# Block 2: where the second half of the output weights is kept and when it and the merged rows are split

## The chip, the core and the metric

The kernel runs on one core of a Trainium2 chip. The engines are TensorE (PE, matmuls, with its weight loads PEld), VectorE (DVE), ScalarE (ACT), GpSimd (POOL) and SyncE (SP, which here issues nearly all DMAs). Each takes its own instructions in order; they meet through semaphores. The metric is the device time of one execution in microseconds. The kernel before takes 2372.64 us, the median of 3 runs (2372.11 to 2374.22).

## The reference, cut to what matters

Two blocks work on 1024 rows of 1024 numbers. The first is a two-layer hybrid of gating and sparse attention; the diff doesn't touch it. The second block normalises its input, projects it, runs a windowed attention and a short gated convolution beside each other, merges them with two gates, projects the sum, adds the input, and sends the result through a mixture of 32 experts. The part that matters is the merge and the output projection:

```python
merged = (jax.nn.sigmoid(g_attn) * (attn @ w_attn_proj[l])
          + jax.nn.sigmoid(g_conv) * (conv @ w_conv_proj[l]))
x = x + merged @ w_out[l]
h2 = rmsnorm(x, norm2_g[l])
x = x + hierarchical_moe(h2, ...)
```

All is float32, and the routing of the experts needs products that are nearly exact.

## The kernel before

Every product is made of three matmuls (`mm3`, lines 99 to 102): each operand is split into a high part, rounded to the matmul's format, and a low part, the rest. `split` (lines 104 to 111) makes the high part on ACT (line 108) or POOL (line 106) and the low part by a subtraction on DVE or POOL (line 111).

The merge (lines 1376 to 1390) runs two branches, first the convolution (`br` 0), then the attention (`br` 1), each over four column groups `dc` of 256. For each group `gate` makes the gate's projection with eight weight tiles k, and ACT turns it into tanh in `sg` (line 1363); then `dense_T(4, ...)` makes the branch's own projection. `ev_p` takes it off PSUM: for branch 0 into the sums M; for branch 1 DVE multiplies into `sg` (line 1388) and POOL adds `sg` to M (line 1389). M lies in the buffer X, one k (128 of the 1024 merged columns) after the other, transposed, so that k is the inner dimension of the output projection: column group `dc` gives k = 2 dc and 2 dc + 1.

Three kinds of place in SBUF matter. `big2` holds two places of tag "s32": first the transposed input's high and low parts, which the gates read until the last gate is through; then `mT`, the split sums of row tiles 0 to 3 and 4 to 7. `gp` has a place of tag "c32" with the split branch input `sT`, which the last projection reads, and after it `w2b`, the second half (k 4 to 7) of the split output weights. `f16` holds the first half, `w2a`, two k per branch.

`load_w2` loads the output weights in parts of one k and 512 columns (256 KB) into two buffers `w2raw`, and splits each: ACT the high, POOL the low part. The first half runs as background work: a generator in the list `bgs`, of which `bg` takes a step whenever its budget is positive; `dense_T` calls `bg` while it emits matmuls, `flush` takes all that is left. The second half is written after the merge (`run(load_w2(4, ...))`), followed by the splits of all eight row tiles, high parts on ACT for even and on POOL for odd tiles.

After that comes the output projection (lines 1550 to 1582). For row tile t it loads the input rows `xt` into a place of X where k 6 or 7 of M lay (line 1552), makes two halves of 24 matmuls each in PSUM banks "half" of which there are three, adds them on DVE (line 1560), starts loads of expert weights into freed places, stores rows, transposes the sum (line 1573) and runs the router. Then the experts follow, with their weights streamed by SP, at most three loads on the way (`AHEAD`).

What sets the order on each engine is not the program's text alone: the building library simulates the program and gives each engine a list, by priority and by its own estimate of when operands are ready. Background steps are emitted at a raised priority (`HI`). So a change in the text can move instructions on every engine behind the place of the change.

Of the kernel before, what the change touches and what calls it, by code (L numbers as in the profile page):

```python
# [11 lines left out]
FR = mybir.dt.float32r  # L12
# [7 lines left out]
OP = mybir.AluOpType  # L20
# [4 lines left out]
S = 1024  # L25
D = 1024
NT = 8
# [13 lines left out]
def tile_hybrid(ctx, tc, I, out):  # L41
    nc = tc.nc
    V, A, G, T = nc.vector, nc.scalar, nc.gpsimd, nc.tensor
# [60 lines left out]
    def split(hi, lo, src, which="pool", sub=None):  # L104
        if which == "pool":
            G.tensor_scalar(hi, src, 1.0, 0.0, op0=OP.mult, op1=OP.add)
        elif which == "act":
            A.activation(hi, src, AF.Copy)  # L108
        else:
            V.tensor_copy(hi, src)  # L110
        return (sub or V).tensor_tensor(lo, src, hi.bitcast(FT), op=OP.subtract)  # L111
# [51 lines left out]
    bgs, streams = [], []  # L163
# [15 lines left out]
    def step(q):  # L179
        try:  # L180
            with tc.high_priority(offset=HI[0]):
                ns = next(q[0])
        except StopIteration:
            q.pop(0)
            return 0.0
        ns, cost = ns if isinstance(ns, tuple) else (ns, 0.0)
        if cost and streams:
            charge(cost)
        return ns
# [32 lines left out]
    def flush(q):  # L222
        while q:
            step(q)
        due[0] = 0.0
# [18 lines left out]
    def dense_T(KT, rhs, evac, bgt=1300.0):  # L244
        ps = [bank([128, 1024], "big") for _ in range(2)]
        for k0 in range(0, KT, 2):
            hi, lo = wnext()
            for f in range(2):
                for kk in range(2):
                    k = k0 + kk  # L250
                    for h in range(2):
                        c = slice(h * 512, (h + 1) * 512)
                        mm3(ps[f][:, c], hi[:, kk, f * 128:(f + 1) * 128], lo[:, kk, f * 128:(f + 1) * 128],
                            rhs(k, 0)[:, c], rhs(k, 1)[:, c], start=(k == 0), stop=(k == KT - 1))
                if k0 + 2 == KT:
                    for h in range(2):
                        evac(f, h, ps[f][:, h * 512:(h + 1) * 512])
                bg(bgt, 12 * 512 / 2.4)
# [222 lines left out]
    def run(g):  # L481
        for _ in g:
            pass
# [638 lines left out]
    big2 = ctx.enter_context(tc.tile_pool(name="big2", bufs=2))  # L1122
# [221 lines left out]
    M = X.rearrange("p t a c -> p (t a c)").rearrange("p (k s) -> p k s", s=S)  # L1344
# [3 lines left out]
    def load_w2(k0, dst):  # L1348
        for kk in range(dst.shape[2]):
            for h in range(2):  # L1350
                raw = gp.tile([128, 512], FT, name="w2raw", bufs=2)
                nc.sync.dma_start(raw, wo2[(k0 + kk) * 128:(k0 + kk + 1) * 128, h * 512:(h + 1) * 512])
                hs = slice(h * 512, (h + 1) * 512)
                split(dst[:, 0, kk, hs], dst[:, 1, kk, hs], raw, "act", G)
                yield 2000.0
        for kk in range(dst.shape[2]):
            w2.append((dst, kk))

    def gate():
        sg = sgpool.tile([128, 2, S], FT, name="sg", tag="sg")  # L1360

        def ev_g(f, h, ps):
            A.activation(sg[:, f, h * 512:(h + 1) * 512], ps, AF.Tanh, scale=0.5)
        dense_T(8, rhs, ev_g)
        return sg

    flush(bgs)
    bank_plan(2, 0, 2, 2)
    sg = gate()
    a2.close()  # L1370
    g2 = ExitStack()
    gp = g2.enter_context(tc.tile_pool(name="gp", bufs=1))
    for br, src in enumerate((convf, attnf)):
        sT = gp.tile([128, 2, 4, S], FR, name="c32")
        for k in range(4):
            split(sT[:, 0, k, :], sT[:, 1, k, :], src[:, k, :], "act")
        bgs.append(load_w2(2 * br, f16.tile([128, 2, 2, S], FR, name="w2a", tag="f16")))
        for dc in range(4):
            if br or dc:
                sg = gate()  # L1380

            def ev_p(f, h, ps):
                hs = slice(h * 512, (h + 1) * 512)
                m = M[:, 2 * dc + f, hs]
                if br == 0:
                    V.scalar_tensor_tensor(m, sg[:, f, hs], 1.0, ps, op0=OP.add, op1=OP.mult)
                else:
                    V.scalar_tensor_tensor(sg[:, f, hs], sg[:, f, hs], 1.0, ps, op0=OP.add, op1=OP.mult)
                    G.tensor_tensor(m, m, sg[:, f, hs], op=OP.add)
            dense_T(4, lambda k, a: sT[:, a, k, :], ev_p)  # L1390
    flush(bgs)
    op = g2.enter_context(tc.tile_pool(name="op", bufs=1))
    run(load_w2(4, gp.tile([128, 2, 4, S], FR, name="w2b", tag="c32", bufs=1)))
    mT = [big2.tile([128, 4, 2, 8, 128], FR, name="s32") for _ in range(2)]
    for t in range(NT):
        m = mT[t // 4][:, t % 4]
        split(m[:, 0], m[:, 1], M[:, :, t * 128:(t + 1) * 128], "pool" if t % 2 else "act")


    h2d = dram.tile([S, D], FT, name="h2d")  # L1400
# [146 lines left out]
    raw0, s32 = [], []  # L1547
    PRE = (0, 1, 1, 1, 1, 1, 1, 1)

    for t in range(NT):  # L1550
        xt = Xf[:, 6 + t % 2]
        nc.sync.dma_start(xt, x2[t * 128:(t + 1) * 128, :])
        for h in range(2):
            hs = slice(h * 512, (h + 1) * 512)
# [159 lines left out]
    with tc.issue_after(late[4].ins):  # L1714
        V.tensor_tensor(ovx[:, 0:NLIM, :], bc(cnt[:, None, :], [128, NLIM, NE]), bc(lim[:, :, None], [128, NLIM, NE]),
                        op=OP.is_gt)
# [53 lines left out]
def build(nc, tc_cls, shapes):  # L1770
    I = {n: nc.dram_tensor(f"in_{n}_dram", a.shape, mybir.dt.from_np(a.dtype), kind="ExternalInput").ap()
         for n, a in shapes.items()}
    out = nc.dram_tensor("out_0_dram", (S, D), FT, kind="ExternalOutput").ap()
    with tc_cls(nc, schedule_with_timeline_sim=True) as tc:
        tile_hybrid(tc, I, out)
# [13 lines left out]
```

## Time and profile before

| what | value |
|---|---|
| median of 3 runs | 2372.64 us (2372.11 to 2374.22) |
| the profiled execution | 2371.94 us |
| its span, first to last instruction | 2369.8 us |
| PE busy | 2140.5 us (90%) |
| DVE busy | 1521.2 us (64%) |
| ACT, POOL busy | 1082.8 us, 1082.0 us (46% each) |
| mean granted TensorE clock | 0.961 |

The shares are means over very different stages: the first block takes most of the span, the merge lies from about 1590 to 1855 us, the output projection until 1983, the experts until the end. Times in the rows are counted from the start of the span. A line number is that of the kernel, and for a helper such as `split` it is the helper's line, so the tile names tell the place: s is any "s32" place, c a "c32" place, whi and wlo a weight tile's high and low part, big and half PSUM banks. What stands in square brackets behind a row is the engine's idle time before it and what ended it.

### The profile page before, as it was taken

Reading aid. Unit: us, or ns where it says so; the run is one execution under the profiler, and the core shown is the slowest. Engines: PE = TensorE matmul, PEld = TensorE weight load, DVE = VectorE, ACT = ScalarE, POOL = GpSimd, SP = SyncE. Lnnn points to the kernel's source line nnn. Section 1 sums busy time; section 2 is a strip of 40 time slices with the busy share of each in tenths; the row PEclk is TensorE's granted clock in tenths of the full one; section 3 lists DMA queues with packets and bytes.
Section 4 is the critical chain, followed back from the end, with each engine's and each line's share of the span. In section 5 each row is a group of like instructions: output and inputs, shape, how many; then the busy total and the mean of one; then the engine's idle time right before and its main releaser. Section 6 shows DMA issues by size and latency. Waiting matters only on the chain. (4 is left out here: it accounts for less than half of the span.)

```text
span 2369.8 us, 35974 instructions
## 1 busy us (share of the span) xinstructions
PE 2140.5 (90%) x13235; PEld 1883.9 (79%) x13235; DVE 1521.2 (64%) x3191; ACT 1082.8 (46%) x1943; POOL 1082.0 (46%) x1018
## 2 busy tenths in 40 slices
PE   5998998798989979997998999999999797999896
PEld 4898897587879979876887888888888586888785
DVE  9768887677753769685776348861010345888784
ACT  4333443554642443436554335652121222778774
POOL 4664575556736553845554345532244412222221
PEclk9999998899999989998999999999999998999998
DMA  7522112312114111223111111122121256999994
GB/s 239 188 79 86 53 32 81 106 59 68 41 47 138 45 36 49 66 67 108 68 45 41 44 41 34 30 52 67 49 67 45 98 209 200 311 325 326 317 329 116
DMA packets 146392, 260.88 MB, mean 110 GB/s; under 512 B 24681, under 2 KB 101889, under 8 KB 133905
## 3 DMA queue, kind: packets, MB, share of 16 engines
q1 hardware_dynamic: 139024, 241.59, 31.1%
q0 software_dynamic: 7168, 16.79, 3.2%
q8 instruction: 105, 1.72, 0.3%
q14 instruction: 95, 0.77, 0.1%
HBM read 228.83 MB, written 37.90 MB: 113 GB/s over the span
## 5 line engine op out<-in xcount | busy, mean ns | idle before, releaser
L111 POOL TENSOR_TENSOR wlo<-wraw,whi 128x512 fp32r<-128x512 f32 (+1 forms) x188 | 249.8, 1329 | 484.9 <-ACT whi L108 459.2
L101 PE MATMUL big<-wlo,s 128*128 128x256 f32 (+1 forms) x1536 | 440.4, 288 | 16.0 <-POOL wlo L111 16.0
L100 PE MATMUL big<-whi,s 128*128 128x256 f32 (+1 forms) x1536 | 437.8, 289 | 13.6 <-ACT s L506 8.4
L102 PE MATMUL big<-whi,s 128*128 128x256 f32 (+1 forms) x1536 | 439.6, 288 | 0.0
L101 PEld LDWEIGHTS big<-wlo,s 128*128 128x128 f32 x1536 | 301.2, 196 | 22.8 <-POOL wlo L111 19.6
L100 PEld LDWEIGHTS big<-whi,s 128*128 128x128 f32 x1536 | 298.6, 196 | 21.9 <-ACT s L506 11.0
L102 PEld LDWEIGHTS big<-whi,s 128*128 128x128 f32 x1536 | 300.6, 196 | 3.1 <-issue 0.9
L108 ACT ACTIVATE whi<-wraw 128x512 fp32r<-128x512 f32 (+1 forms) x188 | 117.7, 627 | 385.2 <-PE big L102 127.2
L111 DVE TENSOR_TENSOR ew<-s,ew 128x1024 fp32r<-128x1024 f32 x138 | 162.8, 1220 | 39.0 <-ACT ew L108 37.9
L636 DVE SCALAR_TENSOR_TENSOR s<-rel,widx,s 128x384 f32<-128x384 f32 (+3 forms) x140 | 130.6, 957 | 85.1 <-ACT rel L631 83.6
L100 PE MATMUL sm<-ew,xT 128*96 128x256 f32 x512 | 147.6, 288 | 4.8 <-ACT xT L1636 4.8
L108 ACT ACTIVATE ew<-s 128x1024 fp32r<-128x1024 f32 x138 | 137.7, 1050 | 28.6 <-PE sm L102 18.8
L102 PE MATMUL sm<-ew,xT 128*96 128x256 f32 x512 | 148.6, 290 | 1.3 <-DVE xT L1637 1.2
L101 PE MATMUL sm<-ew,xT 128*96 128x256 f32 x512 | 146.3, 286 | 0.9 <-DVE ew L111 0.9
L631 ACT ACTIVATE rel<-sm 128x384 f32<-128x384 f32 (+3 forms) x160 | 80.5, 522 | 124.1 <-PE sm L628 114.7
L100 PE MATMUL half<-s,whi 128*128 128x512 f32 x320 | 130.7, 408 | 7.1 <-ACT s L953 3.1
L101 PE MATMUL half<-s,whi 128*128 128x512 f32 x320 | 128.7, 402 | 0.0
L102 PE MATMUL half<-s,wlo 128*128 128x512 f32 x320 | 127.3, 401 | 0.0
L1674 POOL DMA_INDIRECT out_dram<-yt,ti x32 | 58.2, 1820 | 136.0 <-DMA out_dram<-yt,ti 61.0
L606 DVE TENSOR_SCALAR_CACHE_REDUCE bias<-code,cand 128x512 bf16<-128x512 int16 (+5 forms) x126 | 114.1, 924 | 0.5
L878 POOL TENSOR_SCALAR Z<-Z,rc 128x128 f32<-128x128 f32 (+7 forms) x88 | 63.9, 738 | 83.3 <-DVE rc L876 50.7
L100 PE MATMUL big<-s,whi 128*128 128x512 f32 x256 | 99.7, 390 | 0.3 <-DVE convf L1335 0.3
(618 smaller groups left out, 6014.3 us busy)
## 6 DMA issues: line engine op xcount, KB each, us to landing
wraw<-in_w_in_dram SPq DMA_DIRECT2D x164, 256.0 KB, 2.8
adaw<-in_w_ada_dram SPq DMA_DIRECT2D x48, 512.0 KB, 4.5
s<-in_w_gate_e_dram SPq DMA_DIRECT2D x23, 1024.0 KB, 9.2
s<-in_w_up_e_dram SPq DMA_DIRECT2D x23, 1024.0 KB, 11.0
s<-in_w_down_e_dram SPq DMA_DIRECT2D x23, 1024.0 KB, 11.3
X<-in_w_gate_e_dram SPq DMA_DIRECT2D x9, 1024.0 KB, 10.1
X<-in_w_up_e_dram SPq DMA_DIRECT2D x9, 1024.0 KB, 9.8
X<-in_w_down_e_dram SPq DMA_DIRECT2D x9, 1024.0 KB
```

The lines of the kernel that those rows point to most:

```text
L100: T.matmul(o, lh, rh, start=start, stop=False, skip_group_check=True)
L101: T.matmul(o, lh, rl, start=False, stop=False, skip_group_check=True)
L102: T.matmul(o, ll, rh, start=False, stop=stop, skip_group_check=True)
L108: A.activation(hi, src, AF.Copy)
L111: return (sub or V).tensor_tensor(lo, src, hi.bitcast(FT), op=OP.subtract)
L606: V.tensor_scalar(junk[:, :src.shape[1]], src, thr, 0.0, op0=op, op1=OP.add, accum_out=cnt)
L631: A.activation(rel[:, :w_], ps[:, :w_], AF.Relu, scale=0.125)
L636: V.scalar_tensor_tensor(d, rel[:, :w_], widx[:, i, h:h + 1], d, op0=OP.mult, op1=OP.add)
L878: G.tensor_scalar(P[hh][:, :n], P[hh][:, :n], rc[:, hh:hh + 1], 1.0, op0=OP.mult, op1=OP.mult)
L1674: return G.indirect_dma_start(out=out, out_offset=bass.IndirectOffsetOnAxis(ap=ycol, axis=0), in_=yt, in_offset=None, bounds_check=S - 1, ...
```

## The change

`load_w2(4, ...)`, the second half of the output weights, is now put into the second "s32" place, and it becomes background work of the last projection (`br` 1, `dc` 3). So do the splits of row tiles 0 to 3 for k 0 to 5, into the first "s32" place; k 6 and 7 of these tiles are split after the merge. Row tiles 4 to 7 are split in one step as before, but their place is now the "c32" one, that of the branch input. In the last projection DVE, not POOL, adds `sg` to M. POOL makes the high part of tiles 5 and 7 alone; those of 0 to 4 and 6 are ACT's.

```diff
--- before.py
+++ after.py
@@ -1356,6 +1356,14 @@
         for kk in range(dst.shape[2]):
             w2.append((dst, kk))
 
+    mT = []
+
+    def split_m(tiles, a, b):
+        for t in tiles:
+            m = mT[t // 4][:, t % 4, :, a:b]
+            split(m[:, 0], m[:, 1], M[:, a:b, t * 128:(t + 1) * 128], "pool" if t > 3 and t % 2 else "act")
+            yield 1600.0
+
     def gate():
         sg = sgpool.tile([128, 2, S], FT, name="sg", tag="sg")
 
@@ -1378,6 +1386,11 @@
         for dc in range(4):
             if br or dc:
                 sg = gate()
+            last = br == 1 and dc == 3
+            if last:
+                mT.append(big2.tile([128, 4, 2, 8, 128], FR, name="s32"))
+                bgs.append(load_w2(4, big2.tile([128, 2, 4, S], FR, name="s32")))
+                bgs.append(split_m(range(4), 0, 6))
 
             def ev_p(f, h, ps):
                 hs = slice(h * 512, (h + 1) * 512)
@@ -1386,15 +1399,13 @@
                     V.scalar_tensor_tensor(m, sg[:, f, hs], 1.0, ps, op0=OP.add, op1=OP.mult)
                 else:
                     V.scalar_tensor_tensor(sg[:, f, hs], sg[:, f, hs], 1.0, ps, op0=OP.add, op1=OP.mult)
-                    G.tensor_tensor(m, m, sg[:, f, hs], op=OP.add)
+                    (V if last else G).tensor_tensor(m, m, sg[:, f, hs], op=OP.add)
             dense_T(4, lambda k, a: sT[:, a, k, :], ev_p)
     flush(bgs)
+    run(split_m(range(4), 6, 8))
     op = g2.enter_context(tc.tile_pool(name="op", bufs=1))
-    run(load_w2(4, gp.tile([128, 2, 4, S], FR, name="w2b", tag="c32", bufs=1)))
-    mT = [big2.tile([128, 4, 2, 8, 128], FR, name="s32") for _ in range(2)]
-    for t in range(NT):
-        m = mT[t // 4][:, t % 4]
-        split(m[:, 0], m[:, 1], M[:, :, t * 128:(t + 1) * 128], "pool" if t % 2 else "act")
+    mT.append(gp.tile([128, 4, 2, 8, 128], FR, name="mT", tag="c32", bufs=1))
+    run(split_m(range(4, NT), 0, 8))
 
 
     h2d = dram.tile([S, D], FT, name="h2d")
```

In what the engines are given, ACT first, at the last gate and the last projection. Here `big_20520` and `big_20521` are the two PSUM blocks of the last gate, `w2raw` the weight parts, `X_79` the sums M. Before (`w2b_20713` the weights, `s32_20746` and `s32_20747` the split rows):

```order
L1363 ACTIVATE sg_20519<-big_20520 128x512 x2
L108 ACTIVATE whi_20650<-wraw_20648 128x512
L1363 ACTIVATE sg_20519<-big_20521 128x512 x2
L108 ACTIVATE w2b_20713<-w2raw_20714 128x512
L108 ACTIVATE w2b_20713<-w2raw_20718 128x512
L108 ACTIVATE s32_20746<-X_79 128x1024 x2
L108 ACTIVATE w2b_20713<-w2raw_20722 128x512
L108 ACTIVATE s32_20747<-X_79 128x1024 x2
```

Now (`s32_20647` the weights, `s32_20646` the split rows of tiles 0 to 3; line 1363 is now 1371):

```order
L1371 ACTIVATE sg_20519<-big_20520 128x512 x2
L108 ACTIVATE s32_20647<-w2raw_20668 128x512
L108 ACTIVATE s32_20647<-w2raw_20684 128x512
L108 ACTIVATE whi_20652<-wraw_20650 128x512
L108 ACTIVATE s32_20646<-X_79 128x768 x4
L1371 ACTIVATE sg_20519<-big_20521 128x512 x2
L108 ACTIVATE s32_20647<-w2raw_20720 128x512
L108 ACTIVATE s32_20647<-w2raw_20724 128x512
L108 ACTIVATE s32_20647<-w2raw_20728 128x512
L108 ACTIVATE s32_20647<-w2raw_20732 128x512
L108 ACTIVATE s32_20647<-w2raw_20736 128x512
L108 ACTIVATE s32_20646<-X_79 128x256 x4
```

Two weight parts and the four row splits of 768 columns now stand ahead of the second gate block's tanh, and the third to seventh part ahead of the rows' second step of 256 columns.

POOL in the same place, from the first weight tile of the last projection (`wlo_20615`) on. Before:

```order
L111 TENSOR_TENSOR wlo_20615<-wraw_20612,whi_20614 128x512
L111 TENSOR_TENSOR wlo_20651<-wraw_20648,whi_20650 128x512
L1389 TENSOR_TENSOR X_79<-X_79,sg_20519 128x512 x2
L111 TENSOR_TENSOR w2b_20713<-w2raw_20714,w2b_20713 128x512
L1389 TENSOR_TENSOR X_79<-X_79,sg_20519 128x512
L111 TENSOR_TENSOR w2b_20713<-w2raw_20718,w2b_20713 128x512
L1389 TENSOR_TENSOR X_79<-X_79,sg_20519 128x512
L106 TENSOR_SCALAR s32_20746<-X_79 128x1024 x2
```

Now (`mT_20763` the split rows of tiles 4 to 7):

```order
L111 TENSOR_TENSOR wlo_20615<-wraw_20612,whi_20614 128x512
L111 TENSOR_TENSOR s32_20647<-w2raw_20668,s32_20647 128x512
L111 TENSOR_TENSOR s32_20647<-w2raw_20684,s32_20647 128x512
L111 TENSOR_TENSOR wlo_20653<-wraw_20650,whi_20652 128x512
L111 TENSOR_TENSOR s32_20647<-w2raw_20720,s32_20647 128x512
L111 TENSOR_TENSOR s32_20647<-w2raw_20724,s32_20647 128x512
L111 TENSOR_TENSOR s32_20647<-w2raw_20728,s32_20647 128x512
L111 TENSOR_TENSOR s32_20647<-w2raw_20732,s32_20647 128x512
L111 TENSOR_TENSOR s32_20647<-w2raw_20736,s32_20647 128x512
L106 TENSOR_SCALAR mT_20763<-X_79 128x1024 x2
L111 TENSOR_TENSOR s32_20647<-w2raw_20740,s32_20647 128x512
```

The low part of the last projection's second weight tile (`wlo_20651` before, `wlo_20653` now) stands behind two weight parts, the adds of line 1389 are gone, and the eighth part follows the copies of tiles 5 and 7.

DVE from the last projection to the first use of the output projection's sums (`half_...`). Before:

```order
L1388 SCALAR_TENSOR_TENSOR sg_20519<-sg_20519,big_20646 128x512 x2
L1388 SCALAR_TENSOR_TENSOR sg_20519<-sg_20519,big_20647 128x512 x2
L111 TENSOR_TENSOR s32_20746<-X_79,s32_20746 128x1024 x3
L111 TENSOR_TENSOR s32_20747<-X_79,s32_20747 128x1024
L111 TENSOR_TENSOR s32_20746<-X_79,s32_20746 128x1024
L111 TENSOR_TENSOR s32_20747<-X_79,s32_20747 128x1024 x3
L1560 SCALAR_TENSOR_TENSOR X_79<-half_20801,X_79 128x512
```

Now (line 1388 is now 1401, 1389 is 1402, 1560 is 1571, 1573 is 1584):

```order
L111 TENSOR_TENSOR s32_20646<-X_79,s32_20646 128x768 x4
L1401 SCALAR_TENSOR_TENSOR sg_20519<-sg_20519,big_20648 128x512 x2
L1402 TENSOR_TENSOR X_79<-X_79,sg_20519 128x512 x2
L1401 SCALAR_TENSOR_TENSOR sg_20519<-sg_20519,big_20649 128x512 x2
L1402 TENSOR_TENSOR X_79<-X_79,sg_20519 128x512 x2
L111 TENSOR_TENSOR s32_20646<-X_79,s32_20646 128x256 x4
L111 TENSOR_TENSOR mT_20763<-X_79,mT_20763 128x1024 x4
L1571 SCALAR_TENSOR_TENSOR X_79<-half_20809,X_79 128x512
```

Four of the low parts moved ahead of the last projection's multiplications, the adds of M came in between, and twelve instead of eight subtractions make up the rows.

On SP all eight loads of the second half now stand ahead of the loads of the input rows and of the first expert weights; before, the seventh and eighth stood behind these. On PE the last projection's first block of 24 matmuls now runs whole ahead of the second block.

## Rows read from the trace of the kernel before

**Rows 1.** Waits of PE, 1854 to 1990: engine, line, waited for: us, times, longest.
```profile
PE half L100 <- ACT w2b L108: 8.2, 2, 7.8
PE half L100 <- ACT s L108: 4.7, 1, 4.7
```

**Rows 2.** Busy time by window: length, engines' busy us, PEclk, DMA share, GB/s.
```profile
1859.20:1862.40 3.20, 3.16 (x8) 2.49 (x9) 3.19 (x2) 2.24 (x3) 3.20 (x3) 0.50 0.27 82
...
1878.30:1886.10 7.80, 0.00 (x0) 0.00 (x0) 0.00 (x0) 0.63 (x1) 0.00 (x0) 0.79 0.97 374
1886.10:1889.50 3.40, 3.24 (x7) 1.67 (x7) 0.69 (x1) 0.00 (x0) 1.27 (x1) 0.50 0.98 410
...
1905.00:1982.60 77.60, 77.60 (x428) 65.06 (x428) 32.37 (x127) 13.11 (x27) 11.41 (x38) 1.00 0.47 172
...
2100.00:2150.00 50.00, 47.91 (x348) 42.79 (x347) 44.01 (x54) 40.34 (x55) 12.62 (x10) 1.00 0.99 323
...
2070.70:2073.00 2.30, 2.30 (x11) 2.30 (x12) 2.30 (x4) 0.90 (x2) 1.77 (x1) 0.50 1.00 308
1167.60:1169.60 2.00, 2.00 (x9) 1.63 (x10) 1.85 (x6) 0.83 (x1) 1.25 (x1) 1.00 0.95 377
```

**Rows 3.** Timeline of PE: start, length, engine, line, operation, [idle before].
```profile
1843.20 0.39 PE L100 MATMUL big<-c,whi 128*128 128x512 f32 x1
...
1854.17 0.40 PE L102 MATMUL big<-c,wlo 128*128 128x512 f32 x1
...
1889.49 0.73 PE L1573 MATMUL tr<-ident,X 128*128 128x128 f32 x4
```

**Rows 4.** Timeline of SP's DMA queue, 1856 to 1983.
```profile
1876.30 0.80 SPq L1552 DMA_DIRECT2D X<-xs  x2
...
1903.75 0.33 SPq L1552 DMA_DIRECT2D X<-xs  x1
...
1982.69 0.33 SPq L1535 DMA_DIRECT2D s<-in_w_gate_e_dram  x1
```

**Rows 5.** Timeline of ACT, 1843 to 1861.
```profile
1843.23 0.63 ACT L108 ACTIVATE whi<-wraw 128x512 fp32r<-128x512 f32 x1 [1.00 <-issue]
1843.76 1.07 ACT L1363 ACTIVATE sg<-big 128x512 f32<-128x512 f32 x2
...
1858.13 2.00 ACT L108 ACTIVATE s<-X 128x1024 fp32r<-128x1024 f32 x2 [2.37 <-POOL X L1389]
```

**Rows 6.** Timeline of POOL, 1843 to 1869.
```profile
1843.94 1.29 POOL L111 TENSOR_TENSOR wlo<-wraw,whi 128x512 fp32r<-128x512 f32 x1 [4.15 <-ACT whi L108]
...
1856.84 1.26 POOL L1389 TENSOR_TENSOR X<-X,sg 128x512 f32<-128x512 f32 x1
...
1859.28 2.30 POOL L1389 TENSOR_TENSOR X<-X,sg 128x512 f32<-128x512 f32 x1
1861.56 6.99 POOL L106 TENSOR_SCALAR s<-X 128x1024 fp32r<-128x1024 f32 x4
```

**Rows 7.** Timeline of DVE, 1854 to 1908; the third row is the second's latter half.
```profile
1854.67 1.28 DVE L1388 SCALAR_TENSOR_TENSOR sg<-sg,big 128x512 f32<-128x512 f32 x2 [1.02 <-PE big L102]
1859.21 3.45 DVE L111 TENSOR_TENSOR s<-X,s 128x1024 fp32r<-128x1024 f32 x2 [3.26 <-ACT s L108]
...
1860.36 2.30 DVE L111 TENSOR_TENSOR s<-X,s 128x1024 fp32r<-128x1024 f32 x1
...
1907.60 0.69 DVE L1560 SCALAR_TENSOR_TENSOR X<-half,X 128x512 f32<-128x512 f32 x1 [2.16 <-DMA X<-xs]
```

**Rows 8.** Groups of DVE by form: line, shapes, xcount | busy us, mean ns.
```profile
L111 DVE TENSOR_TENSOR c<-convf,c 128x1024 fp32r<-128x1024 f32 x4 | 4.6, 1221 | 0.3 <-ACT c L108 0.3
```

**Rows 9.** The page's DMA issues: xcount, KB each, median us to landing.
```profile
wraw<-in_w_in_dram SPq DMA_DIRECT2D x164, 256.0 KB, 2.8
```

**Rows 10.** Timeline of PE behind two gaps elsewhere in the program.
```profile
2070.69 0.59 PE L1658 MATMUL tr<-ident,th 96*128 96x96 f32 x2 [2.23 <-DVE xT L1637]
...
1167.54 0.50 PE L100 MATMUL half<-s,yah 128*128 128x512 f32 x1 [2.57 <-DVE s L1045]
```

## Prediction

> **What bounds the kernel now.** I read the waits of TensorE (PE) first, around the place that the diff touches: after the last projection PE waited 8.2 us for ACT's splits of the second half of the output weights (w2b), 7.8 of it at once, and 4.7 us for the first split rows of the merged activations [rows 1]. The windows show the same by stage: PE idles through 1878.3 to 1886.1, runs at a granted clock of 0.50 in the stretches behind its two long gaps, is busy at 1.00 without a gap from 1905 to 1982.6, and from 2100 on shares the time with DMA engines that are busy to 0.99 [rows 2]. So PE's order bounds the stage from 1843 to 1983, and only what it loses before 1890 can be got back.
>
> How much that is: the last projection's 48 matmuls start at 1843.20 (first) and 1854.17 (last), 47 steps of 0.2334 us; the next could start at 1854.40. The first transposes of row tile 0 start at 1889.49 [rows 3], and in PE's order 69 output matmuls stand ahead of them. These need 69 x 0.2334 = 16.1 us and took 35.1: **19.0 us are lost**.
>
> Whether a gain there reaches the end: the first load of the expert stage goes out at 1982.69, after the last output matmul [rows 4], and everything from there hangs on it. A whole stage that starts earlier ends earlier, though its DMA is full.
>
> **The change part by part.** All times below are on the clock of the profiled execution; up to 1843.2 nothing in the order moves.
>
> *ACT.* At 1843.2 both places of the transposed input come free. ACT now issues two w2b parts, then the last weight tile of the projection (whi), four row splits of 768 columns, and only then the second gate half (sg). Starts of 512-column splits lie 0.53 apart (1843.23, 1843.76), two of 1024 take 2.00 [rows 5]; 768 columns so take about 0.75. That gives whi at 1844.29 (before: 1843.23), row splits 1844.82 to 1847.8, sg done 1848.9 (before: 1844.8). PE's second block of projection matmuls waits for sg, but in the new order the whole first block (5.6 us from 1843.20) runs ahead of it, so that delay is covered.
>
> *POOL and DVE.* POOL's low part of the last weight tile (wlo) ran at 1843.94 for 1.29 [rows 6]; now two w2b parts stand ahead of it. Here the two engines hold each other up: the first 1024-column DVE subtraction took 3.45 - 2.30 = 1.15 us, the second 2.30 [rows 7], and POOL's add beside the first took 2.30 where the one before it took 1.26; a DVE subtraction of that size with POOL still takes 1.22 [rows 6, 8]. They take turns: whoever comes second waits for the whole of the other. In such turns a DVE split costs 0.9 (768 columns), 0.35 (256), 1.15 (1024), an add of 512 columns 0.62 (by columns), a POOL part 1.2, a POOL copy of 1024 columns 0.9 (four in 6.99 with DVE between). POOL's first w2b part ends at 1845.2, the second at 1846.46, DVE's first row split takes the turn to 1847.35, wlo ends at 1848.55. PE needs it at 1843.20 + 14 x 0.2334 = 1846.47: **stall of 2.1 us**. Without turns it is 1.3, with wlo and a part both slowed 2.9.
>
> The Trainium skill ("SBUF — State Buffer", section "SBUF: two separate sides") calls this an exclusive lock, held for a whole instruction, of a DVE operation with two SBUF inputs against a GpSimd operation that reads SBUF. By that rule the adds that the diff moves to DVE take turns too, which speaks against moving them, and no row of before shows such an add on DVE; without it the stall is 1.3, the transposes below wait for nothing, and the sum is about 15 instead of 14.
>
> *Hand-over.* The projection's matmuls now end with the step at 1856.5. The first output matmul, as the program is built, waits for the second half's multiplications (line 1388, now 1401); they began 0.1 after the last matmul's end and took 1.28 for two [rows 7]. That is 1858.0: **1.5 us** of gap. Before, this wait was over at 1855.95 and hidden by the 4.7 us for the splits. Now it is what is late: tiles 0 to 3 have k 0 to 5 split by 1852.4. All output matmuls queue behind it.
>
> *Weights.* A 256 KB weight load lands in 2.8 us [rows 9], and a new one goes out when POOL is done with its buffer: parts 3 to 8 land from 1848 to 1861. The eighth part's low half comes last, at 1864.8, behind POOL's two row copies; its matmul is number 47 of the output, due at 1858.0 + 46 x 0.2334 = 1868.7. So both waits of [rows 1] go to nothing, and the two loads that before stood on SP behind the first expert load are ahead of it now.
>
> *Second step of the rows.* k 6 and 7 of tiles 0 to 3 need the last sums: projection end 1856.7, two multiplications, two adds: 1859.3. ACT splits from there; DVE's low halves take turns with POOL. Used first by output matmul 24, due 1863.4; the first is done at about 1861. Tiles 4 to 7 follow on DVE, 4 x 1.15 after POOL's last part: end at 1869.9. As a check, the turns from 1843.9 sum to DVE 4 x (0.9 + 0.62 + 0.35 + 1.15) = 12.1 and POOL 9 x 1.2 + 2 x 0.9 = 12.6, so 1868.6 if never idle.
>
> *SP.* The input rows of row tiles 0 and 1 go where k 6 and 7 of the sums lie, so their loads wait for that last DVE split: 1876.30 before [rows 4], 1869.9 now. A row load went out at 1903.75 and DVE waited for it until 1907.60 [rows 4, 7]: 3.85. Then line 1560 (now 1571) at 1873.75, 0.69 long; transposes at 1874.4. PE has 68 output matmuls ahead of them, over at 1858.0 + 15.9 = 1873.9: **0.5 us**, and 0.2 more before the second four transposes. Bounds: 0 if the splits don't take turns (1867), 6 if they end as late as before. All matmuls and the router stand behind these transposes.
>
> *Clock.* After the gap of 4.7 [rows 1] PE ran at 0.50, the 1.2 GHz level, for 3.2 us, which cost 1.6. A gap of 2.23 was followed by 0.50, one of 2.57 by 1.00, the 2.4 GHz level [rows 2, 10]. The new gap of 2.1 is of that size: bounds 0 and 1.6, I take 0.8.
>
> **Sum:** 19.0 - 2.1 - 1.5 - 0.7 - 0.8 = 13.9, say 14 us. One matmul more or less ahead of the transposes is in the rounding. The profiled execution took 2371.94 (span 2369.8 and 2.1 around it), the median is 0.7 above it: 2371.94 - 14 + 0.7 = **2358.6 us**.
>
> **Rivals.**
> 1. *Longer new stalls.* Wlo late by 2.9, the clock down (1.6), the row load as late as before (1876.3 + 3.85 + 0.7 = 1880.9, 7 us behind PE). For it: POOL and DVE do the same work in either kernel, and before it ended at 1876.3. Against: it starts 11 us earlier (1843.2 for 1854.6). These add up only in part, since a later PE waits less at the transposes: 19 - 2.9 - 1.6 - 1.5 - 5 = 8: 2364.6.
> 2. *Hardly a stall.* Wlo 1.3, no clock loss, transposes on time: 19 - 2.8 = 16.2: 2356.4; the floor with nothing lost is 2353.6.
> 3. *Nothing is left.* The expert stage runs at the DMA's pace [rows 2]; were its end set by something that doesn't move, it would be 2372.6. Against: its loads start only when the output matmuls have left their buffer [rows 4], and that moves.
> 4. *Slower.* The row load of tile 2 needs tile 0's store to be through, which now stands behind two row loads and three expert loads that start 6 us earlier: 4.2 MB at 374 to 410 GB/s [rows 2] is 11 us, so the store ends near 1886 and the load lands near 1890. On DVE its use (line 1571 for tile 2) stands ahead of the routing of tiles 0 and 1, on PE its transposes are due at about 1895. From then on each us is lost one for one on PE. To be slower by 0.2% it would have to land 19 us after that. The Trainium skill ("DMA: Bandwidth & Descriptors", "Queues, rings and completion order") has descriptors consumed in ring order, which is why I let the store wait for all that is ahead; no run here shows this store under that load.
>
> **How the numbers follow.** About 0.2% (4.7 us) is what a measurement of this kernel can tell from no change. Forecast (10.5 to 16 us gained) 0.72, rival 1 0.15, rival 2 0.06, rival 3 0.04, rival 4 0.03. Faster 0.93, same 0.04, slower 0.03. The range holds the forecast, rival 2 nearly to its floor and most of rival 1: 2354 to 2366.
>
> **What would show it.** In the profile after: PE's waits for w2b and for s (the split rows) are gone; a new wait of PE for POOL wlo at about 1846.5 of 1 to 3 us; one for DVE sg (line 1401) of about 1.5; one for DVE X or the row load ahead of line 1584 of under 2. The SP load of the row tiles goes out at about 1870, the first expert load behind the output projection at about 1968 to 1969, and the rest shifts by the same. I am wrong if PE still waits for weights after 1860, if the row load goes out as late as 1876, or if new waits appear between 1880 and the end of the output matmuls.

## The result and the profile after

The changed kernel takes 2356.39 us (median of 6 executions, 2351.19 to 2362.38), the one before in the same comparison 2372.38 (6, 2370.26 to 2374.27): ratio 0.993, 95% interval 0.9914 to 0.9945. It is 16.0 us faster; 2358.6 was forecast, with 2354 to 2366 as range. The profiled execution took 2353.97 (span 2352.3).

First the waits of PE in the profile after, from 1830 to 1990 (engine, line, waited for: us, times, longest):

```profile
PE tr L1645 <- DMA X<-h2d,ti: 8.4, 1, 8.4
PE sm L1497 <- DVE OH L1495: 4.7, 1, 4.7
PE big L102 <- POOL wlo L111: 1.8, 1, 1.8
PE half L100 <- DVE sg L1401: 1.5, 1, 1.5
PE sm L1595 <- POOL OHc L1503: 1.0, 1, 1.0
```

Both waits of [rows 1] are gone. The rows of lines 1645, 1497 and 1595 stand behind the last output matmul, where the kernel before waits too (7.5, 5.3 and 1.0 us). In front of that there are two new ones, at the places forecast: 1.8 us for wlo (2.1 forecast) and 1.5 for the hand-over of PSUM (1.5), for which PE waits until DVE has read the projection's last sums. No wait stands in front of the transposes of row tile 0 (line 1584), where 0.7 was forecast. PE's timeline shows where they lie (start, length, engine, line, operation, idle before and what ended it):

```profile
1843.73 0.39 PE L100 MATMUL big<-c,whi 128*128 128x512 f32 x1
...
1848.96 0.50 PE L102 MATMUL big<-c,wlo 128*128 128x512 f32 x1 [1.80 <-POOL wlo L111]
...
1856.76 0.40 PE L102 MATMUL big<-c,wlo 128*128 128x512 f32 x1
1858.70 0.47 PE L100 MATMUL half<-w2a,s 128*128 128x512 f32 x1 [1.54 <-DVE sg L1401]
...
1874.24 0.49 PE L1584 MATMUL tr<-ident,X 128*128 128x128 f32 x3
```

The first row is the start of the last projection, called P0 from here. Its own time differs between traces although nothing in front of it was touched, so every later time is counted from it. Before, the transposes began 1889.49 - 1843.20 = 46.3 us behind P0 [rows 3], now 1874.24 - 1843.73 = 30.5.

SP's rows answer to [rows 4]:

```profile
1869.62 0.80 SPq L1563 DMA_DIRECT2D X<-xs  x2
...
1874.31 0.34 SPq L1579 DMA_DIRECT2D out_dram<-X  x1
...
1885.65 0.32 SPq L1563 DMA_DIRECT2D X<-xs  x1
...
1964.97 0.33 SPq L1546 DMA_DIRECT2D s<-in_w_gate_e_dram  x1
```

The row loads go out at 1869.6 (1869.9 forecast, 1876.30 before), the first expert load behind the output at 1965.0 (1968 to 1969 forecast). Between them are the store of row tile 0 and the row load of tile 2. The timelines of POOL, ACT and DVE around the stall, one after the other:

```profile
1844.41 2.55 POOL L111 TENSOR_TENSOR s<-w2raw,s 128x512 fp32r<-128x512 f32 x2 [4.10 <-ACT s L108]
1846.92 1.98 POOL L111 TENSOR_TENSOR wlo<-wraw,whi 128x512 fp32r<-128x512 f32 x1
```

```profile
1844.76 0.62 ACT L108 ACTIVATE whi<-wraw 128x512 fp32r<-128x512 f32 x1
1845.28 3.03 ACT L108 ACTIVATE s<-X 128x768 fp32r<-128x768 f32 x4
1848.22 1.06 ACT L1371 ACTIVATE sg<-big 128x512 f32<-128x512 f32 x2
```

```profile
1846.21 6.35 DVE L111 TENSOR_TENSOR s<-X,s 128x768 fp32r<-128x768 f32 x4 [22.71 <-ACT s L108]
...
1857.26 1.28 DVE L1401 SCALAR_TENSOR_TENSOR sg<-sg,big 128x512 f32<-128x512 f32 x2 [2.30 <-PE big L102]
1858.47 1.29 DVE L1402 TENSOR_TENSOR X<-X,sg 128x512 f32<-128x512 f32 x2
1859.71 5.28 DVE L111 TENSOR_TENSOR s<-X,s 128x256 fp32r<-128x256 f32 x4
1864.92 4.62 DVE L111 TENSOR_TENSOR mT<-X,mT 128x1024 fp32r<-128x1024 f32 x4
1872.99 1.29 DVE L1571 SCALAR_TENSOR_TENSOR X<-half,X 128x512 f32<-128x512 f32 x2 [3.45 <-DMA X<-xs]
```

Wlo runs behind the two parts of w2b, beside DVE's first row split, and takes 1.98 in place of 1.29 [rows 6]. The last row ends at 1874.28, where PE's transposes begin: row load and PE arrive together, which decides most of the experiments.

### The profile page after: what moved, and what is told of

It reads as the page before. It is cut to its first block, busy times and chain, and to the rows that moved or that the text cites. A ratio compares the mean times of both kernels' runs of the same rounds, so it can differ in the third digit from the quotient of the medians.

```text
span 2352.3 us, 35985 instructions
## 1 busy us (share of the span) xinstructions
PE 2139.3 (91%) x13235; PEld 1886.7 (80%) x13235; DVE 1526.4 (65%) x3199; ACT 1085.8 (46%) x1949; POOL 1070.6 (46%) x1012
## 5 line engine op out<-in xcount | busy, mean ns | idle before, releaser
L636 DVE SCALAR_TENSOR_TENSOR s<-rel,widx,s 128x384 f32<-128x384 f32 (+3 forms) x140 | 125.5, 922 | 80.8 <-ACT rel L631 79.4
L100 PE MATMUL sm<-ew,xT 128*96 128x256 f32 x512 | 149.7, 292 | 4.5 <-ACT xT L1647 4.3
L108 ACT ACTIVATE ew<-s 128x1024 fp32r<-128x1024 f32 x138 | 137.7, 1049 | 30.5 <-PE sm L102 26.7
L102 PE MATMUL sm<-ew,xT 128*96 128x256 f32 x512 | 150.1, 293 | 0.7 <-DVE xT L1648 0.6
L101 PE MATMUL sm<-ew,xT 128*96 128x256 f32 x512 | 148.1, 289 | 0.9 <-DVE ew L111 0.9
L1685 POOL DMA_INDIRECT out_dram<-yt,ti x32 | 53.1, 1660 | 129.4 <-DMA out_dram<-yt,ti 54.5
```

Source lines behind the costliest of these rows:

```text
L100: T.matmul(o, lh, rh, start=start, stop=False, skip_group_check=True)
L101: T.matmul(o, lh, rl, start=False, stop=False, skip_group_check=True)
L102: T.matmul(o, ll, rh, start=False, stop=stop, skip_group_check=True)
L636: V.scalar_tensor_tensor(d, rel[:, :w_], widx[:, i, h:h + 1], d, op0=OP.mult, op1=OP.add)
L1685: return G.indirect_dma_start(out=out, out_offset=bass.IndirectOffsetOnAxis(ap=ycol, axis=0), in_=yt, in_offset=None, bounds_check=S - 1, ...
```

## The experiments

All were measured beside the kernel before, in three comparisons (e1 to e4, e5 to e8, e9 to e12). The median is that of n executions; the other columns are from the one execution that was profiled, those behind P0 in us from it, read from PE's and SP's timelines: row loads out, transposes of tile 0, end of the last output matmul, end of the span.

| kernel | median (n) | P0 | row loads | transposes | output over | end |
|---|---|---|---|---|---|---|
| before | see below | 1843.2 | 33.1 | 46.3 | 139.5 | 526.7 |
| changed | 2356.39 (6) | 1843.7 | 25.9 | 30.5 | 121.2 | 508.5 |
| e1 changed again | 2358.59 (6) | 1844.8 | 27.0 | 32.0 | 122.7 | 509.3 |
| e2 rows in one step | 2357.93 (6) | 1847.7 | 29.0 | 36.3 | 126.0 | 512.5 |
| e3 rows only | 2370.98 (12) | 1844.2 | 27.9 | 45.9 | 136.9 | 523.8 |
| e4 adds on POOL | 2357.43 (5) | 1846.1 | 28.2 | 33.0 | 122.7 | 512.4 |
| e5 wlo first | 2353.13 (6) | 1841.6 | 25.1 | 29.3 | 120.4 | 506.0 |
| e6 free bank | 2352.51 (6) | 1842.8 | 27.3 | 32.6 | 121.7 | 502.9 |
| e7 e5 + e6 | 2355.59 (6) | 1845.6 | 27.9 | 32.1 | 121.3 | 507.4 |
| e8 e7 + split order | 2359.08 (7) | 1848.1 | 27.6 | 38.3 | 126.4 | 513.2 |
| e9 changed, third | 2354.66 (6) | 1842.8 | 27.0 | 32.1 | 122.7 | 509.3 |
| e10 last sums first | 2350.17 (6) | 1842.5 | 20.6 | 27.0 | 119.3 | 502.7 |
| e11 no priority, bank | 2350.13 (5) | 1841.2 | 24.9 | 28.9 | 120.6 | 506.0 |
| e12 e11 + e10's order | 2351.58 (6) | 1841.7 | 19.9 | 27.1 | 119.7 | 507.1 |

Before took 2373.12 (17), 2373.42 (12) and 2372.33 (11) in the three comparisons. The traces tell apart 1 us at the place of the change; the medians don't, since P0 alone spreads over 7 us.

**e1 and e9, the changed kernel again.** No edit.

> The changed kernel once more, unchanged. Theory: on PE the same two gaps in front of 1859 as in its first trace (1.8 us for POOL wlo, 1.5 for DVE sg) and the transposes of row tile 0 within 0.5 us of 1874.2; median between 2353 and 2360. What spreads its times from 2351 to 2362 lies behind the first expert load, where the DMA engines are full. Rival: the spread lies in the new gaps (wlo 1.3 to 2.9, a clock drop of 1.6 behind it); then the transposes of tile 0 move by 1 us or more from trace to trace, by as much as the whole.

> The changed kernel a third time, as the measure for the next three. Theory: the stall of 1.8 us for wlo again, with or without half clock behind it; transposes of row tile 0 at P0 + 30.5 or P0 + 32.0 (P0 is the start of the last projection), median 2354 to 2359. Rival: another value of the stall.

Medians 2358.59 and 2354.66. The stall is 1.8 in all three traces, but behind it the clock differs. The window behind the stall of e1, then of e9 (length, busy us of PE, PEld, DVE, ACT, POOL, PEclk, DMA share, GB/s):

```profile
1850.40:1853.40 3.00, 3.00 (x9) 2.32 (x8) 3.00 (x3) 1.06 (x2) 2.49 (x2) 0.50 0.01 5
```

```profile
1848.60:1851.60 3.00, 3.00 (x9) 2.35 (x8) 2.98 (x3) 0.87 (x2) 2.69 (x2) 0.50 0.00 1
```

and the same place in the first trace of the changed kernel:

```profile
1849.00:1851.00 2.00, 2.00 (x9) 1.64 (x10) 2.00 (x3) 1.43 (x3) 1.13 (x1) 1.00 0.09 33
```

PE ran at 1.2 GHz (half clock, a PEclk of 0.50) for 3 us in two of the three, and its transposes came 1.5 us later in these. On the spread both theories were off: behind the first expert the three traces take 366.8 to 367.3 us, the clock accounts for 1.5, and P0 varies by 2 among these three, by 7 among all.

**e2, only w2b early.** `split_m(range(4), 0, 6)` is not put into `bgs`; the rows of tiles 0 to 3 are split whole:

```diff
-                bgs.append(split_m(range(4), 0, 6))
-    run(split_m(range(4), 6, 8))
+    run(split_m(range(4), 0, 8))
```

> Only the first part of the change: the second half of the output weights (w2b) early in the second s32 place, but tiles 0 to 3 of the rows split whole, after the last sums. Theory: no row split of DVE stands beside wlo any more, so wlo takes 1.3 instead of 2.0 and the stall falls from 1.8 to about 1.1; but the first output matmul waits 2 to 4.5 us longer than now for tile 0's split, and DVE has 3.6 to 6.4 us more to do behind the last sums, so that the row loads go out at 1873 to 1876 and the transposes come 4 to 6.5 us later: 2360 to 2363. Rival (the early row split only moves work about, since DVE and POOL are the bound anyway): within 1 us of the changed kernel, 2356.4.

The waits of PE for rows, and POOL's wlo:

```profile
PE half L100 <- ACT s L108: 5.9, 1, 5.9
```

```profile
1850.85 1.29 POOL L111 TENSOR_TENSOR wlo<-wraw,whi 128x512 fp32r<-128x512 f32 x1
```

The wait for the split rows is back, with half clock behind it; the transposes come 4.2 to 5.8 us later than in the changed kernel, the end 3.2 to 4.0. The median, 0.7 below e1's, can't show that: this profiled execution was the slowest of its six. So the trace bears the theory out, and the time decides nothing: the median also lies under the 2360 to 2363 expected. Against the theory there is no stall for wlo at all (1.1 expected). Without row splits in front of it ACT starts sg at P0 + 1.6 (P0 + 4.5 in the changed kernel), PE alternates between the halves of the projection (14, 14, 10, 10 matmuls, before as well) and needs wlo 14 matmuls later. Taking the early row splits away thus removes the stall, and two things change with them: DVE no longer stands beside wlo (1.29 for 1.98), and sg no longer stands behind the splits on ACT. They don't make the stall alone. In e3, which has them without the early w2b, wlo takes 2.01 as well, but sg starts at P0 + 3.5, PE alternates and never waits for wlo. That the time of sg is what turns PE's order is inferred from these traces; no run changed it alone.

**e3, only the rows early.** w2b stays behind the merge:

```diff
-                bgs.append(load_w2(4, big2.tile([128, 2, 4, S], FR, name="s32")))
-    mT.append(gp.tile([128, 4, 2, 8, 128], FR, name="mT", tag="c32", bufs=1))
+    run(load_w2(4, gp.tile([128, 2, 4, S], FR, name="w2b", tag="c32", bufs=1)))
+    mT.append(big2.tile([128, 4, 2, 8, 128], FR, name="s32"))
```

> Only the other part: rows of tiles 0 to 3 in two steps, but w2b loaded and split after the last projection, into the c32 place, and tiles 4 to 7 in the second s32 place. Theory: no stall for wlo, the hand-over gap of 1.5 stays, and PE waits 10 to 13 us for w2b, since its last two loads stand on SP behind the row loads again: 4 to 6 us faster than before, 2366 to 2368. Rival (the 4.7 us wait for the split rows with its clock drop was what mattered): 2358 to 2361.

```profile
PE half L100 <- ACT w2b L108: 12.0, 1, 12.0
PE half L100 <- DVE sg L1400: 1.6, 1, 1.6
PE big L100 <- ACT whi L108: 0.6, 1, 0.6
```

and POOL's wlo:

```profile
1847.78 2.01 POOL L111 TENSOR_TENSOR wlo<-wraw,whi 128x512 fp32r<-128x512 f32 x1 [7.04 <-ACT whi L108]
```

12.0 us for w2b, as the theory had it; ratio 0.9989 (0.9978 to 1.0), 2.1 us faster than before by the medians and 2.8 from P0 to the end, less than the 4 to 6 expected: half clock followed the wait, which I had not counted, and PE waited 0.9 for whi and sg, which stand behind the row splits on ACT. At the transposes only 0.4 of the gain is there, with 72 output matmuls in front of them where 69 stood. Nearly all of the gain so needs w2b beside the last projection: that alone (e2) gives 526.7 - 512.5 = 14 of the 17 to 18 us from P0 to the end.

**e4, the last adds left on POOL.**

```diff
-                    (V if last else G).tensor_tensor(m, m, sg[:, f, hs], op=OP.add)
+                    G.tensor_tensor(m, m, sg[:, f, hs], op=OP.add)
```

> The change with the last four adds left on POOL. Theory: 4 adds of 1.3 to 2.3 us come into POOL's row, the second step of the row splits starts 1 to 2.5 us later, and so do the row loads (1870.6 to 1872) and the transposes: 2357.5 to 2359. Rival (by turns DVE pays for POOL's adds whichever engine does them): no difference, transposes at 1874.2 and 2356.4.

The row loads go out 1.2 us later than in e1 (both with half clock), as expected, but the scheduler put 72 output matmuls ahead of the transposes where 68 stood, and the output is over at P0 + 122.7 in both. This is the result that the rival named, though nothing here shows its reason: moving the adds gained nothing that can be measured. The later end comes from a longer wait behind the output, for the gather of rows (11.3 us, in e1 7.2 at the longest), not pursued.

**e5, wlo first.** The background steps beside the last projection at a priority below the weights':

```diff
             if last:
+                HI[0] = 80
```

> Times counted from the start of the last projection (P0), since its own time drifts by 4 us between traces. In the changed kernel the transposes of row tile 0 stand at P0 + 30.5 (clock up) or 32.0 (clock down after the stall), the end at P0 + 508.5 to 509.3. Here the last weight tile's split (whi, then wlo on POOL) goes ahead of the two w2b parts. Theory: the 1.8 us stall for wlo is gone and with it the chance of a clock drop; but the row load of tile 0 then comes last, since DVE and POOL have the same splits to do, so that PE waits 0.5 to 1.8 us in front of the transposes: P0 + 29 to 30.2, end P0 + 507.5 to 508.5. Rival (PE alone sets it): no wait there, transposes at P0 + 28.7.

```profile
PE half L100 <- DVE sg L1402: 1.5, 1, 1.5
PE tr L1585 <- DVE X L1572: 1.0, 1, 1.0
```

The stall is gone, and in its place PE waits 1.0 us in front of the transposes, which come at P0 + 29.3. That is the theory, with an end 1.5 us earlier than it had: the wait that I forecast there (0.7) exists, and in the changed kernel the stall covered it. The ratio to the kernel before is 0.9912 (0.989 to 0.9934), an interval that overlaps the changed kernel's 0.9914 to 0.9945.

**e6, e7, e8: a free bank.** For the first half of row tile 0 (e6), with `HI[0] = 80` (e7), and with the row splits of tiles 4 to 7 in two steps too (e8):

```diff
-            py = bank([128, 512], "half")
+            py = bank([128, 512], "half" if t or h else "sm")
```
```diff
-    run(split_m(range(4), 6, 8))
-    run(split_m(range(4, NT), 0, 8))
+    run(split_m(range(NT), 6, 8))
+    run(split_m(range(4, NT), 0, 6))
```

> The first half of row tile 0's output gets a PSUM bank of the kind sm, which is free, in place of one that the last projection hands over; the scheduler then puts output matmuls beside the projection's. Theory: the gap of 1.5 us for DVE sg is gone or covered, but the row load of tile 0 goes out no earlier (1869.6, P0 + 25.9), so PE waits 1 to 2 us in front of the transposes instead: P0 + 30.5 with the clock up, no gain. Rival (PE alone sets it): P0 + 29.0, end 1.5 us earlier than now.

> Both of the last two. Theory: no gap on PE before the transposes' own wait, which takes their place with 1.5 to 3 us: transposes at P0 + 28.7 to 30.2, end P0 + 507 to 508.5. Rival (PE alone): P0 + 27.2, end P0 + 505.5.

> Both, and the rows of tiles 4 to 7 in two steps as well (k 6 and 7 of all tiles in one piece of the program, k 0 to 5 of tiles 4 to 7 as soon as the c32 place is free), so that DVE has work while it waits for the last sums. Theory: the row loads go out at P0 + 22 to 24 in place of P0 + 25.9 and the transposes come at P0 + 27 to 28.7, the end at P0 + 505.5 to 507, 2 to 4 us faster than the changed kernel. Rival (the smaller pieces cost DVE and POOL as much as the filled gap gives): transposes at P0 + 29 or later, no better than with both edits alone.

None moved the end of the output forward against e5. The scheduler put 18 output matmuls between those of the projection, so that the last sums came later, and the hand-over gap of 1.5 stayed, now in front of the second half. In e6 the row loads went out at P0 + 27.3 and the output was over at P0 + 121.7: no gain, as the theory said, but not by its wait of 1 to 2 us in front of the transposes. With 84 output matmuls ahead of them, where 68 stood, PE waited for nothing there, and they came at P0 + 32.6. For e7 (transposes at 32.1) theory and rival were both too early. For e8 (38.3) the rival's "29 or later" came out, but not for its reason, as SP's timeline shows:

```profile
1873.06 0.33 SPq L1547 DMA_DIRECT2D X<-in_w_gate_e_dram  x1
1873.43 0.43 SPq L1547 DMA_DIRECT2D X<-in_w_up_e_dram  x1
1873.90 0.43 SPq L1547 DMA_DIRECT2D X<-in_w_down_e_dram  x1
1875.77 0.80 SPq L1564 DMA_DIRECT2D X<-xs  x2
```

and on DVE:

```profile
1885.67 0.69 DVE L1572 SCALAR_TENSOR_TENSOR X<-sm,X 128x512 f32<-128x512 f32 x1 [10.01 <-DMA X<-xs]
```

Three expert loads got in front of the row loads, since DVE split k 0 to 5 of the sums first, which frees the places of the expert weights. The row load took 9.9 us from issue to use (3.4 in the changed kernel), and PE waited 3.3 and fell to half clock. This is the mechanism of my rival 4, at another load than the one it named.

**e10, the last sums first.** e5, and k 0 to 5 of tiles 4 to 7 made to wait for the last split of k 6 and 7:

```diff
+    run(split_m(range(NT), 6, 8))
+    run(split_m(range(4, NT), 0, 6, lows[-1]))   # follow(high part, lows[-1])
```

> Wlo first as in e5, and k 6 and 7 of all eight row tiles split before k 0 to 5 of tiles 4 to 7, so that the row loads wait for 8 splits of 256 columns and no longer for 4 of 1024. Theory (the way from the last sums over the splits and the row load to the transposes is the second limit): row loads at P0 + 21 to 23 in place of e5's 25.1, PE's wait of 1.0 in front of the transposes gone, transposes at P0 + 28.3, end about 1 us before e5's P0 + 506.0. Rival (POOL's late parts of w2b become the limit): a new wait of PE for w2b of 1 us or more, no gain on e5.

```profile
PE half L100 <- DVE sg L1411: 1.5, 1, 1.5
```

```profile
1863.00 0.80 SPq L1573 DMA_DIRECT2D X<-xs  x2
1868.51 0.33 SPq L1556 DMA_DIRECT2D X<-in_w_gate_e_dram  x1
```

One wait is left on PE up to 1960. The row loads go out at P0 + 20.6, 4.5 us before e5's and 5.5 ahead of the expert loads; the output is over 1.1 us before e5's, about what was expected of the end. So the path from the last sums over the splits and the row load is the second limit, shown by moving it. The end itself comes 3.3 before e5's; the other 2.2 lie behind the output, and no experiment explains them.

**e11 and e12.** `HI[0] = 0`, so that the background steps beside the last projection have no raised priority at all, and the free bank (e11); the same with e10's order of splits (e12).

> The steps beside the projection without raised priority, so that wlo and the second gate half (sg) go ahead of w2b and of the row splits, and a free bank for the first output half. In the program no output matmul stands between the projection's any more, and 18 stand between its end and the first that needs a handed-over bank. Theory: no gap on PE from P0 to the transposes but their own; projection over at P0 + 11.2, output from there; row loads as in e5 (P0 + 25), so that PE waits 2 to 3 us there: transposes at P0 + 29 to 30, no better than e5. Rival (PE alone sets it): transposes at P0 + 27.4.

> e11 with the splits in the order of e10: both limits moved. Theory: row loads at P0 + 21 to 23, transposes at P0 + 26.5 to 28, end at P0 + 503.5 to 505, 3 to 5 us ahead of the changed kernel. Rival (something else is late, POOL's last w2b parts): a wait of 1 us or more for w2b and no better than e5.

In e11 PE has no gap until the transposes and waits 0.8 us there, less than expected: P0 + 28.9, the output over at 120.6 (e5 120.4), so no better than e5. In e12 PE has no gap above 0.05 us from P0 to the last output matmul, and yet the output is over at P0 + 119.7, 0.4 later than e10's with its gap of 1.5: in e12 the 16 router matmuls of tile 6 (1.5 us) stand in front of that end, in e10 behind it. The first expert's transposes come at P0 + 138.5 in e12, 140.4 in e10, 141.7 to 142.4 in the changed kernel. The end, P0 + 507.1, missed the 503.5 to 505 expected, since the experts took 368.5 us. With PE dense no idle time is left to win in front of the routing.

By trace e10 is 1.8 to 3.4 us ahead of the changed kernel where the output is over. In its comparison its median is 2350.17 with ratio 0.9908 (0.9892 to 0.9924), e11's and e12's 2350.13 and 2351.58, the changed kernel's 2354.66 with 0.9929 (0.991 to 0.9949). They beat the kernel before; against the changed one the intervals overlap.

## Why the prediction was right

**PE's order bounds the stage, and what it lost came back.** Right: e12 runs it dense, and e3, with the wait for w2b left in, gains 2 us and not 16. None of the three signs of being wrong came: no wait for weights after 1860, the row load at 1869.6, no gap on PE from the transposes to the last output matmul.

**Weights and rows.** Both waits of [rows 1] went to nothing. That the early w2b carries nearly all was left open; e2 and e3 show it: 14 of 17 to 18 us.

**Stall for wlo.** 2.1 forecast, 1.8 in four traces (the changed kernel's three and e4). The account by turns holds: with DVE's row splits beside it wlo takes 1.98 (2.01 in e3), without them 1.29 (e2). The Trainium skill ("SBUF — State Buffer", section "SBUF: two separate sides") describes an exclusive lock between a DVE operation with two inputs in SBUF and a GpSimd operation that reads SBUF, and these rows agree. I named only POOL's order and the turns as the reason. That PE takes the first half whole I had as cover for sg; it is also what makes wlo due 14 matmuls earlier than in e2 and e3, where PE alternates and doesn't wait for wlo.

**Hand-over.** The gap was forecast at 1.5 and measured 1.54.

**Transposes.** A wait of 0.7 was forecast and none measured: the row load took 3.4 from issue to use where I had put 3.85, and the stall held PE back. E5 shows 1.0 there as soon as the stall is gone. The two terms are not a sum: whichever is longer hides the other.

**Clock.** I took 0.8 between 0 and 1.6. A single execution has either: 0 in one trace of the changed kernel, 1.5 in two.

**The sum.** From P0 to the transposes the gain is 46.3 - 30.5 = 15.8 without the clock drop and 14.3 with it; 14 was forecast. One term was missing: I had nothing move behind the transposes. From them to the end of the output the stage took 93.2 us before and 90.7 after, 1.7 of it because tile 6's router matmuls fell behind the last output matmul (11.63 us of router matmuls in this stretch before, 9.96 after). Up to 1.1 comes back in the wait for the routing. These 2.5 and the 1.8 by which 15.8 exceeds 14 put the first expert load at 1965.0 and not at 1968 to 1969. From P0 to the end of the span the gain is 17.3 to 18.1 us, and the medians give 16.0, 14.5 and 17.7 in the three comparisons, with P0 adding its own few us to each. That 2358.6 came within 2.2 of the median is thus partly luck: P0 alone moves a single execution by up to 7.

**Rivals.** Of rival 1 only the clock came, in some executions. Rival 2's short stall didn't come: 1.8 lies between its 1.3 and the 2.1 forecast. Rival 3 fell: the experts take 365.5 to 368.5 us from their first transposes in twelve of fourteen traces, whenever they start. Rival 4's load was no limit here: the row load of tile 2, which waits for tile 0's store (issued at 1874.31), went out at 1885.65, near the 1886 forecast, and PE waited for nothing at its transposes. Its mechanism is real, as e8 shows.

Open: e6 and e10 take 361.4 and 362.4 us there, 3 to 7 less than the other twelve; nothing run here says why, and their ends and medians gain by it.

## What to carry to other kernels

When a wait is taken off the critical engine, write down which chain arrives next and by how much; two new waits one behind the other are not a sum, since the first covers the second. Moving preparation beside an earlier stage costs where it stands in front of that stage's own operands: put it below them in priority (in e5 one line took away 1.8 us of stall, and no clock drop followed there; 1.0 came back as a wait in front of the transposes). Let small loads that something waits for go out before large ones: the same row load took 3.4 us from issue to use in front of three loads of 1 MB and 9.9 behind them. Where the program drifts by more than the effect, compare traces from an event just before the change.

## What was unexpected of the hardware

- A gap on PE of 1.8 us was followed by half clock in 3 of 4 traces (e1, e4, e9, not the first), at a cost of 1.5 us; the hand-over gap of 1.5 to 1.6 us was not in any of ten. The length of the gap alone doesn't decide: some 1470 us earlier in the program PE waits 1.38 to 1.39 us in every trace, and half clock followed in 11 of 14, as in the first of the changed kernel (PE's row, then a window behind it):

```profile
380.74 0.50 PE L100 MATMUL half<-s,whi 128*128 128x512 f32 x1 [1.39 <-ACT s L953]
```

```profile
381.30:383.80 2.50, 2.50 (x7) 1.94 (x7) 2.39 (x7) 2.47 (x5) 2.50 (x3) 0.50 0.90 352
```

- The same instructions in front of P0 took 1841.2 to 1848.1 us in fourteen traces. Among the three of the changed kernel that is 2.0, and from P0 to the end they differ by 0.8.
- DVE's adds with two operands in SBUF took 1.28 for two alone in e5, and 2.40 beside a part of w2b on POOL (last row):

```profile
1851.56 1.28 DVE L1403 TENSOR_TENSOR X<-X,sg 128x512 f32<-128x512 f32 x2
...
1854.38 2.40 DVE L1403 TENSOR_TENSOR X<-X,sg 128x512 f32<-128x512 f32 x2
```

```profile
1854.83 1.39 POOL L111 TENSOR_TENSOR s<-w2raw,s 128x512 fp32r<-128x512 f32 x1 [0.73 <-ACT s L108]
```
